# Walking the second MLP matrix in pairs of column blocks, and turning thirteen more tiles by DMA

## The chip, the cores and the metric

The kernel runs on one core of a Trainium2 chip. The metric is the time of one execution on the device in microseconds; the kernel before has a median of 1602.38 us over 3 runs (1599.79 to 1604.03). One more execution was taken with the hardware profiler, and its rows are what is quoted here. In them PE is the matmul engine (PEld its weight load), DVE the vector engine, ACT the scalar engine, POOL GpSimd, and SP the engine that issues most DMAs.

## The reference

One decoder block on x of 256 rows by 2048 columns, in float32:

```python
h = rms_norm(x, ln1_g[l])
proj = h @ w_in[l]                    # split into 12 parts
o_attn = dsa_attention(aq, ak, av, iq, ik, iw, topk)      # aq, ak: rms_norm per head
o_ret = silu(rg) * group_norm_heads(retention_chunkwise(...))
merged = sigmoid(ga) * (o_attn @ w_up_attn[l]) + sigmoid(gb) * (o_ret @ w_up_ret[l])
x = x + merged @ w_out[l]
h2 = rms_norm(x, ln2_g[l])
x = x + square(relu(h2 @ w_ff1[l])) @ w_ff2[l]
```

w_ff1 is 2048 x 8192 and w_ff2 is 8192 x 2048. The attention has 16 query heads and 4 key heads of 128 columns, and each query keeps the 64 keys of the highest indexer score.

## The kernel before

**Products.** Every float32 product is made of three matmuls on a high and a low part: high x high (L406), high x low part of the weights (L407), low part of the activations x high (L408). The weights come from HBM by DMA in tiles of 1 MB (`raw`, `rawc`), issued by SP, are rounded to the high part by ACT (`whi`, L360), and DVE subtracts to get the low part (`wlo`, L361). The activations are split likewise, after they have been transposed: ACT L430 writes the high, DVE L431 the low part of four 128x128 blocks at a time into the pair `act` that PE reads.

**Two ways to transpose.** `transpose_in` puts four 128x128 blocks of a tile through PE with an identity (L463) into a PSUM bank, and splits from there. `turn_in` calls `turned`: ACT copies the tile into two planes of 16 bits (L441), SP issues a transposing DMA from SBUF to SBUF (L443), and ACT copies the planes back together (L447); then the tile is split. `heads_T` (L557) turns keys and queries on PE. Each of these is a generator in a work list; `step()` is called once per item of the products and advances every generator in the list by one `yield`, so `wait` and `land` in the code count items.

**The MLP.** The 8192 columns of w_ff1 are taken in 8 groups (`NG`) of 1024. The first product of a group is formed, from group 1 on, with seven half-size products in place of eight (two levels of sums of weight tiles, which DVE adds in place: L350, the table `SUMS`), and is written to `pq` banks; its seven products have four items each. The second product (w_ff2, F2) of group g-1 runs in between: 16 items, for four column blocks `i` of 512 by two halves `h` by two steps `s`; an F2 item is 12 matmuls, a first-product item 6. `merged(g)` makes the list: one F2 item after every two items of the first product. An F2 block collects in two `pf` banks (one for each of the two row tiles t). At its last item ACT evicts each bank with a scale into a tile `ev` (L1261, two buffers), and POOL issues a DMA that adds it to `sums` in HBM (L1262). `F2_HALVES = (1, 0)`: of each block the half with the tiles (t, 1) comes first, then that of the tiles (t, 0).

A group makes four tiles (t, i), t and i 0 or 1, each squared after a relu by `squared` (L1178, L1179). `hidden(g, t, i)` puts them into the work list: in groups 1 to 6 the tiles (0,1), (1,1) and (0,0) go by `turn_in` and (1,0) by `transpose_in`; in group 7 (0,0) goes by `transpose_in` too; in group 0 all four do.

**The order.** The program is written in one order; a planner with costs for each instruction sets the order of each engine's instructions, and pools of a fixed number of buffers set what may be in flight.

Of the kernel before, what the change touches and what calls it, by code (L numbers as in the profile page):

```python
# [10 lines left out]
F32 = mybir.dt.float32  # L11
# [3 lines left out]
AF = mybir.ActivationFunctionType  # L15
# [3 lines left out]
P = 128  # L19
D = 2048  # L20
S = 256
T = S // P
DK = D // P
BN = 512
# [9 lines left out]
KC, HC = 4, 2  # L34
FG = 8
NG = DFF // (FG * P)
# [84 lines left out]
F2_HALVES = (1, 0)  # L121


def merged(g):

    f = iter([("F2", g - 1, i, h, s) for i in range(D // BN) for h in F2_HALVES for s in range(KC // HC)])
    out = []
    for n, p in enumerate(ORDER):
        for h in range(HK // KC):
            out += [("Q", g, n, h, s) for s in range(KC // HC)]  # L130
            if g > 1 or (n, h) > (0, 0):
                out.append(next(f))
        if p == 4:
            out.append(next(f))
    return out + list(f)
# [25 lines left out]
def block_kernel(ctx, tc, cst, rot, xt, gains, w, x, ret_gn_g, ret_gn_b, out):  # L161
    nc = tc.nc
# [9 lines left out]
    ep = tc.alloc_tile_pool(name="ep", bufs=1, side="right", reuse_waits="tile")  # L172
# [16 lines left out]
    banks(**ONE)  # L189


    W_NORM, W_SOFT, W_GN, W_CROSS, W_LATE = 3, 5, 7, 8, 10
    n_stg, n_mid, n_sm = 8, {"ep": 12, "e4": 20}, 24
    late = {"ep": ep, "stg": ep}
    n_stage = [0]
# [1 line left out]
    def nm(s):  # L197
        uid[0] += 1
        return f"{s}_{uid[0]}"

    def stage(shape=(P, BN)):
        n_stage[0] += 1
        pool, bufs = (late["stg"], 2) if n_stage[0] % 4 == 0 and "stg" in late else (sp, n_stg - 2)
        return pool.tile(list(shape), F32, tag="stg", name=nm("stg"), bufs=bufs)

    def mid(shape, dtype=F32):
        return late["ep"].tile(list(shape), dtype, tag="mid", name=nm("mid"), bufs=n_mid[late["ep"].name])

    def small(w):
        return sp.tile([P, w], F32, tag="small", name=nm("small"), bufs=n_sm)  # L210

    def psum_t():
        return PS["pt"].tile([P, BN], F32, tag="pt", name=nm("pt"))
# [8 lines left out]
    work = []  # L222
# [14 lines left out]
    gq, gk = gT[:, 2 * DK:2 * DK + 1], gT[:, 2 * DK + 1:2 * DK + 2]  # L237
# [32 lines left out]
    for g in range(1, NG):  # L270
        use += merged(g)
# [142 lines left out]
    def rsqrt(v, n, mul):  # L414

        a, y, u = small(n), small(n), small(n)
        nc.vector.tensor_scalar(a, v, mul, EPS, op0=ALU.mult, op1=ALU.add)
        nc.vector.tensor_scalar(y.bitcast(I32), a.bitcast(I32), -0.5, float(0x5F3759DF), op0=ALU.mult, op1=ALU.add)
        for _ in range(3):
            nc.vector.tensor_tensor(u, y, y, op=ALU.mult)  # L420
            nc.vector.scalar_tensor_tensor(u, u, -0.5, a, op0=ALU.mult, op1=ALU.mult)
            nc.vector.scalar_tensor_tensor(y, u, 1.5, y, op0=ALU.add, op1=ALU.mult)
        return y

    def split_into(act, k0, nk, t, ps):

        src = ps.rearrange("p (c i) -> p c i", c=nk)
        hi = act[0][:, k0:k0 + nk, t * P:(t + 1) * P]
        lo = act[1][:, k0:k0 + nk, t * P:(t + 1) * P]
        nc.scalar.activation(hi, src, AF.Copy)  # L430
        nc.vector.tensor_tensor(lo, src, hi.bitcast(F32), op=ALU.subtract)  # L431

    def interleaved(a):
        return a.bitcast(U16).rearrange("p (j h) -> p h j", h=2)

    def planes(a):
        return a.bitcast(U16).rearrange("p (h j) -> p h j", h=2)

    def turned(src, halves, wait):

        nc.scalar.activation(planes(halves), interleaved(src), AF.Copy)  # L441
        yield
        nc.sync.dma_start_transpose(src.bitcast(U16).rearrange("p (c r) -> p c r", r=P), halves.bitcast(U16))  # L443
        for _ in range(wait):
            yield
        with tc.issue_after(late["split"]):
            nc.scalar.activation(interleaved(halves), planes(src), AF.Copy)  # L447

    def turn_in(act, k0, t, src, tile_for, wait, land=W_CROSS):

        for _ in range(wait):
            yield
        halves = tile_for((P, BN))
        yield from turned(src, halves, land)
        split_into(act, k0, 4, t, halves)

    def transpose_in(act, k0, t, src, wait=2):

        for _ in range(wait):
            yield  # L460
        ps = psum_t()
        for c in range(4):
            nc.tensor.transpose(ps[:, c * P:(c + 1) * P], src[:, c * P:(c + 1) * P], ident)  # L463
        split_into(act, k0, 4, t, ps)
# [19 lines left out]
    psK, psI = ([PS["pm"].tile([P, BN], F32, tag="pm", name=nm("pm")) for _ in range(T)] for _ in range(2))  # L484
# [14 lines left out]
    def evict(dst, ps, t, func=AF.Copy):  # L499
        nc.scalar.activation(dst, ps, func, scale=rows[t])  # L500

    def evicted(ps, t):
        a = stage()
        evict(a, ps, t)
        return a
# [28 lines left out]
    def row_heads(tiles):  # L534

        hs = small(4 * T)
        for t, a in enumerate(tiles):
            sq = stage()
            nc.scalar.activation(sq, a, AF.Square)
            nc.vector.tensor_reduce(hs[:, 4 * t:4 * t + 4], sq.rearrange("p (h d) -> p h d", h=4), axis=AX.X, op=ALU.add)  # L540
        yield
        r = rsqrt(hs, 4 * T, 1.0 / HD)
        yield
        for t, a in enumerate(tiles):
            av = a.rearrange("p (h d) -> p h d", h=4)
            nc.vector.tensor_tensor(av, av, r[:, 4 * t:4 * t + 4].unsqueeze(2).to_broadcast([P, 4, HD]), op=ALU.mult)
        return tiles

    def heads_T(norm, dsts, g, wait):

        tiles = yield from norm
        for _ in range(wait):
            yield
        for t, a in enumerate(tiles):
            pst = psum_t()
            for h in range(4):
                nc.tensor.transpose(pst[:, h * P:(h + 1) * P], a[:, h * P:(h + 1) * P], ident)  # L557
            pst, dst = pst.rearrange("p (h i) -> p h i", h=4), dsts[t]
            if isinstance(dst, list):
                nc.scalar.activation(dst[0], pst, AF.Copy, scale=g)  # L560
                nc.vector.scalar_tensor_tensor(dst[1], pst, g, dst[0].bitcast(F32), op0=ALU.mult, op1=ALU.subtract)
            else:
                nc.scalar.activation(dst, pst, AF.Copy, scale=g)
            yield

    kT = ep.tile([P, NKV, S], F32, tag="kT", name="kT")
    vv = px.tile([P, 2, T, NKV * HD], F32R, tag="big2", name="vv")
    work.append(heads_T(row_heads([evicted(psK[t], t) for t in range(T)]), [kT[:, :, t * P:(t + 1) * P] for t in range(T)], gk, 2 * W_NORM))

    iqs = ep.tile([P, T, IW], F32, tag="big", name="iqs")  # L570
    for i in range(3):
# [84 lines left out]
    scale = HD ** -0.5  # L656
# [259 lines left out]
    for gate, u in ((z, u) for z in BESIDE for u in range(2)):  # L916
# [10 lines left out]
        for item in beside(gate, u):  # L927
# [7 lines left out]
            else:  # L935
                branch(item, of(oT if gate == "GA" else hT))
                i = item[0][1] - 2 * u
# [87 lines left out]
    for j in range(4):  # L1025
        if j < 2:

            i = j
# [5 lines left out]
        for src in (ret_gn_g, ret_gn_b):  # L1034
            g = mid([P, BN])
# [35 lines left out]
    for i in range(4):  # L1071
        ms = mss[i] if i in pair else gates(i)
        ps = run_block(("UR", i), of(rT), ps=pair.get(i), k0=len(PARTS[0]) * KC if i in pair else 0)
        for t, m in enumerate(ms):
            g = sgb[:, t, i * BN:(i + 1) * BN]
# [106 lines left out]
    def put(*new):  # L1182
        for (t, i), z, src in new:
            ys[t, i] = squared(z, src)
        for (t, i), _, _ in new:
            hidden(g, t, i)
# [3 lines left out]

    def hidden(g, t, i):
        act, y = [z[:, g % 2 * FG:] for z in hid[:2]], ys.pop((t, i))
        if g and (i or t == 0 and g < NG - 1):
            wait, room = ((1, 3)[t], spread) if i else (2, stage)
            work.append(turn_in(act, 4 * i, t, y, room, wait, W_LATE))
        else:
            work.append(transpose_in(act, 4 * i, t, y, 4 if g and (t, i) == (1, 0) else 2))

    def spread(shape):
        return late["f2"].tile(list(shape), F32, tag="stg", name=nm("halves"), bufs=2)  # L1200
# [3 lines left out]
    for i in (1, 0):  # L1204
        ps = run_block(("F1", i), lambda k, t: form(blocks[k // HK][t], k % HK))
        for t in range(T):
            ys[t, i] = squared(stage(), ps[t])
            if i:
                hidden(0, t, i)
# [58 lines left out]
    for t in range(T):  # L1268
        hidden(0, t, 0)
    for g in range(1, NG):  # L1270
        b, e = {}, {}
        for item in merged(g):
            if item[0] == "F2":
                second(item)
            else:
                first(item, b, e, form, put)
# [37 lines left out]
```

## Time and profile before

| what | value |
|---|---|
| median of 3 runs | 1602.38 us |
| profiled execution | 1600.71 us, span 1598.9 us |
| granted TensorE clock | 1.000 |
| PE busy | 1591.0 us |
| PE weight load busy | 1316.9 us |
| DVE busy | 1308.4 us (82%) |
| ACT busy | 1077.8 us (67%) |
| POOL busy | 90.6 us |
| HBM | 219 GB/s over the span |

The page of the profile gives for each engine the busy time and its share of the span, then the span in 40 slices, the DMA queues, the chain that ended last, and the costliest groups of instructions: line, engine, operation, tile written <- tiles read, shape, count, then busy time, mean duration in ns, and idle time of the engine before them with its releaser. The timelines have one row an instruction: start and duration in us, engine, line, operation and tiles. PE's matmuls overlap in their pipeline, so what one costs is read from start to start, and not from its duration.

### The profile page before, as it was taken

What the parts mean: (1) busy time and instruction counts of PE and PEld (TensorE: products, weight loads), DVE (VectorE), ACT (ScalarE), POOL (GpSimd) and SP (SyncE); (2) the same over time, 40 slices, a digit from 0 to 9 for tenths busy, and PEclk for the clock granted to TensorE, in tenths of its full rate; (3) what the DMA queues carried; (4) which work ended last, traced back from release to release, by engine and by line L of the source; (5) the groups of instructions that cost most, each with busy time, mean ns of one, the idle gap of its engine ahead of it and who ended that gap; (6) DMA issues with size and microseconds to landing.
All of it is one profiled execution on the core that took longest, in us unless ns stands there. A gap on an engine that the chain in (4) does not pass through costs nothing.

```text
span 1598.9 us, 19614 instructions
## 1 busy us (share of the span) xinstructions
PE 1591.0 (100%) x7294; PEld 1316.9 (82%) x7294; DVE 1308.4 (82%) x1466; ACT 1077.8 (67%) x1382; POOL 90.6 (6%) x135
## 2 busy tenths in 40 slices
PE   9999999999999999999999999999999999999999
PEld 8978888888888888888888888888887878888887
DVE  6678779898989898688575589898989898989884
ACT  7556766766566666466574666777878786868672
POOL 0000000000000001202000000000000000000000
PEclk9999999999999999999999999999999999999999
DMA  9645347856565755877666574878787777878773
GB/s 329 220 155 182 135 155 241 263 224 232 196 256 206 268 194 182 323 222 276 212 238 247 198 274 146 261 202 269 216 254 216 249 242 237 256 237 257 215 214 136
DMA packets 106432, 361.23 MB, mean 226 GB/s; under 512 B 45792, under 2 KB 52576, under 8 KB 70752
## 3 DMA queue, kind: packets, MB, share of 16 engines
q1 hardware_dynamic: 89056, 318.40, 56.8%
q0 software_dynamic: 14256, 35.14, 10.4%
q10 hardware_dynamic: 3024, 6.44, 1.1%
q8 instruction: 57, 0.93, 0.2%
q14 instruction: 39, 0.32, 0.1%
HBM read 323.24 MB, written 27.26 MB: 219 GB/s over the span
## 4 chain that ended last, share of the span: by engine, by line
PE 87%; DVE 8%; issue 2%; ACT 2%; DMA 1%; ACTq 0%; DVEq 0%
PE pm L407 11%; PE pm L408 11%; PE pm L406 11%; PE pf L407 9%; PE pf L408 9%; PE pf L406 9%; PE pq L407 7%; PE pq L408 7%; PE pq L406 7%; DVE wlo L361 4%; DVE raw L350 3%; ACT whi L360 1%; DMA rawc<-in_w_dram 1%; ACT halves L447 1%; DVE act L431 1%
## 5 line engine op out<-in xcount | busy, mean ns | idle before, releaser
L361 DVE TENSOR_TENSOR wlo<-raw,whi 128x1024 fp32r<-128x1024 f32 (+2 forms) x544 | 643.9, 1201 | 202.3 <-ACT whi L360 194.5
L360 ACT ACTIVATE whi<-raw 128x1024 fp32r<-128x1024 f32 (+2 forms) x544 | 561.3, 1042 | 348.2 <-PE pm L408 159.3
L406 PE MATMUL pm<-whi,act 128*128 128x512 f32 (+1 forms) x800 | 308.9, 387 | 1.5 <-ACT act L474 1.5
L407 PE MATMUL pm<-wlo,act 128*128 128x512 f32 (+1 forms) x800 | 306.9, 384 | 0.2 <-DVE wlo L361 0.2
L408 PE MATMUL pm<-whi,act 128*128 128x512 f32 (+1 forms) x800 | 307.1, 384 | 0.0
L407 PE MATMUL pf<-wlo,act 128*128 128x512 f32 (+1 forms) x768 | 299.0, 389 | 0.5 <-DVE wlo L361 0.5
L408 PE MATMUL pf<-whi,act 128*128 128x512 f32 (+1 forms) x768 | 298.6, 389 | 0.0
L406 PE MATMUL pf<-whi,act 128*128 128x512 f32 (+1 forms) x768 | 298.2, 390 | 0.4 <-ACT act L430 0.3
L361 DVE TENSOR_TENSOR wlo<-rawc,whi 128x1024 fp32r<-128x1024 f32 x176 | 215.0, 1221 | 41.2 <-ACT whi L360 39.0
L360 ACT ACTIVATE whi<-rawc 128x1024 fp32r<-128x1024 f32 x176 | 186.2, 1058 | 73.7 <-PE pf L408 35.1
L350 DVE TENSOR_TENSOR raw<-raw,raw 128x2048 f32<-128x2048 f32 x88 | 201.1, 2287 | 0.5
L406 PEld LDWEIGHTS pm<-whi,act 128*128 128x128 f32 x800 | 150.3, 188 | 28.2 <-ACT act L474 1.7
L408 PEld LDWEIGHTS pm<-whi,act 128*128 128x128 f32 x800 | 150.4, 188 | 27.9 <-DVE act L475 0.2
L407 PEld LDWEIGHTS pm<-wlo,act 128*128 128x128 f32 x800 | 150.5, 188 | 27.7 <-DVE wlo L361 1.9
L407 PEld LDWEIGHTS pf<-wlo,act 128*128 128x128 f32 x768 | 144.2, 188 | 31.7 <-DVE wlo L361 2.7
L406 PEld LDWEIGHTS pf<-whi,act 128*128 128x128 f32 x768 | 143.7, 188 | 32.3 <-ACT whi L360 2.3
L408 PEld LDWEIGHTS pf<-whi,act 128*128 128x128 f32 x768 | 144.2, 188 | 31.6 <-DVE act L431 2.2
L407 PE MATMUL pq<-wlo,xf 128*128 128x512 f32 x392 | 153.2, 391 | 0.8 <-DVE wlo L361 0.8
L406 PE MATMUL pq<-whi,xf 128*128 128x512 f32 x392 | 152.8, 390 | 0.0
L408 PE MATMUL pq<-whi,xf 128*128 128x512 f32 x392 | 152.6, 389 | 0.0
L1262 POOL DMA_DIRECT2D sums<-ev x56 | 48.1, 936 | 757.1 <-ACT ev L1261 755.4
L407 PEld LDWEIGHTS pq<-wlo,xf 128*128 128x128 f32 x392 | 73.6, 188 | 18.3 <-DVE wlo L361 3.2
(223 smaller groups left out, 1575.0 us busy)
## 6 DMA issues: line engine op xcount, KB each, us to landing
raw<-in_w_dram SPq DMA_DIRECT2D x188, 1024.0 KB, 5.5
rawc<-in_w_dram SPq DMA_DIRECT2D x88, 1024.0 KB, 5.2
sums<-ev POOLq DMA_DIRECT2D x56, 256.0 KB, 5.3
raw<-in_w_dram SPq DMA_DIRECT2D x8, 736.0 KB, 4.9
raw<-in_w_dram SPq DMA_DIRECT2D x7, 512.0 KB, 7.0
raw<-in_w_dram SPq DMA_DIRECT2D x8, 368.0 KB, 7.4
stg<-in_x_dram SPq DMA_DIRECT2D x8, 256.0 KB, 7.6
mgd<-stg POOLq DMA_DIRECT2D x8, 256.0 KB, 5.8
```

Of the source, the lines that this page charges most:

```text
L350: nc.vector.tensor_tensor(one, one, two, op=ALU.add)
L360: late["split"] = nc.scalar.activation(a, src, AF.Copy).ins
L361: nc.vector.tensor_tensor(b, src, a.bitcast(F32), op=ALU.subtract)
L406: nc.tensor.matmul(d, h, hi, start=first, stop=False, skip_group_check=skip)
L407: nc.tensor.matmul(d, h, lo, start=False, stop=False, skip_group_check=skip)
L408: nc.tensor.matmul(d, l, hi, start=False, stop=last, skip_group_check=skip)
L431: nc.vector.tensor_tensor(lo, src, hi.bitcast(F32), op=ALU.subtract)
L447: nc.scalar.activation(interleaved(halves), planes(src), AF.Copy)
L1262: nc.gpsimd.dma_start(sums[:, t, i * BN:(i + 1) * BN], z, accum_op=ALU.add)
```

## The change

Three things are changed. `merged` walks the column blocks of F2 in pairs: for two blocks first both halves of the tiles (t, 1), then both of the tiles (t, 0), so four `pf` banks are open at once, and blocks end with the 6th, 8th, 14th and 16th F2 item instead of the 4th, 8th, 12th and 16th. The half h = 0 of a group is first read by the 5th F2 item instead of the 3rd. `hidden` sends all tiles but (1,0) of group 7 through `turn_in`, with new waits and new numbers of items for the landing. The two key tiles go through `turned` in a new pair of generators. In all, 52 PE transposes (13 sets of four) go; 26 ACT copies and 13 transposing DMAs on SP come.

```diff
-    f = iter([("F2", g - 1, i, h, s) for i in range(D // BN) for h in F2_HALVES for s in range(KC // HC)])
+    f = iter([("F2", g - 1, i + a, h, s) for i in range(0, D // BN, 2) for h in F2_HALVES for a in range(2) for s in range(KC // HC)])
...
-    W_NORM, W_SOFT, W_GN, W_CROSS, W_LATE = 3, 5, 7, 8, 10
+    W_NORM, W_SOFT, W_GN, W_CROSS = 3, 5, 7, 8
...
-    work.append(heads_T(row_heads([evicted(psK[t], t) for t in range(T)]), [kT[:, :, t * P:(t + 1) * P] for t in range(T)], gk, 2 * W_NORM))
+
+    def key_heads(tiles):
+
+        yield from row_heads(tiles)
+        for _ in range(W_NORM):
+            yield
+        for t, a in enumerate(tiles):
+            work.append(key_tile(t, a))
+
+    def key_tile(t, a):
+
+        for _ in range(2 * t):
+            yield
+        halves = ep.tile([P, BN], F32, tag="halves", name=nm("halves"), bufs=2)
+        yield from turned(a, halves, W_CROSS)
+        nc.scalar.activation(kT[:, :, t * P:(t + 1) * P], halves.rearrange("p (h i) -> p h i", h=4), AF.Copy, scale=gk)
+
+    work.append(key_heads([evicted(psK[t], t) for t in range(T)]))
...
         act, y = [z[:, g % 2 * FG:] for z in hid[:2]], ys.pop((t, i))
-        if g and (i or t == 0 and g < NG - 1):
-            wait, room = ((1, 3)[t], spread) if i else (2, stage)
-            work.append(turn_in(act, 4 * i, t, y, room, wait, W_LATE))
-        else:
-            work.append(transpose_in(act, 4 * i, t, y, 4 if g and (t, i) == (1, 0) else 2))
+        if g == NG - 1 and (t, i) == (1, 0):
+            work.append(transpose_in(act, 4 * i, t, y, 4))
+            return
+        wait, room, land = (1 + 2 * t, spread if g or not i else stage, 10 if not g else 7)
+        if g and not i:
+            wait, room, land = ((2, stage, 15), (1, spread, 11))[t] if g < NG - 1 else (1, stage, 7)
+        work.append(turn_in(act, 4 * i, t, y, room, wait, land))
```

The planner sets the order of each engine anew. Two places are shown, both at the start of an MLP group in the middle (the profile of before has it at 1214 us).

ACT, before: the splits of weights (`whi`) of the first items, the copies (L447) and splits (L430) of the tiles (0,1) and (1,1), one relu and square (L1178, L1179), and the evictions (`ev`) of the last block.

```order
L360 ACTIVATE whi_10726<-raw_10651 128x1024
L447 ACTIVATE halves_10566<-stg_10449 128x2x512
L360 ACTIVATE whi_10742<-raw_10651 128x1024
L430 ACTIVATE act_7813<-halves_10566 128x4x128
L1178 ACTIVATE stg_10537<-stg_10537 128x512
L1179 ACTIVATE stg_10537<-stg_10537 128x512
L360 ACTIVATE whi_10758<-rawc 128x1024
L447 ACTIVATE halves_10596<-stg_10289 128x2x512
L1261 ACTIVATE ev_10777<-pf_10657,q_7814 128x512
L430 ACTIVATE act_7813<-halves_10596 128x4x128
L1261 ACTIVATE ev_10780<-pf_10658,q_7814 128x512
L360 ACTIVATE whi_10784<-raw_10695 128x1024
```

The same place after (lines are moved: the relu is L1195 and the square L1196, the eviction L1280; the first L447 and its L430 stand just ahead of these rows, with the first eviction):

```order
L1280 ACTIVATE ev_10705<-pf_10494,q_7812 128x512
L360 ACTIVATE whi_10710<-rawc 128x1024
L447 ACTIVATE halves_10589<-stg_10279 128x2x512
L360 ACTIVATE whi_10723<-raw_10638 128x1024
L430 ACTIVATE act_7811<-halves_10589 128x4x128
L1195 ACTIVATE stg_10528<-stg_10528 128x512
L360 ACTIVATE whi_10736<-raw_10638 128x1024
L1196 ACTIVATE stg_10528<-stg_10528 128x512
L360 ACTIVATE whi_10752<-rawc 128x1024
L441 ACTIVATE halves_10756<-stg_10528 128x1024
L1280 ACTIVATE ev_10770<-pf_10559,q_7812 128x512
L1280 ACTIVATE ev_10773<-pf_10560,q_7812 128x512
```

The next row is `whi_10777`, which answers to `whi_10784` before. Ahead of it there are now two pairs of evictions instead of one, and the first copy (L441) of the tile (1,0).

DVE, before: the adds (L350), the splits of weights (`wlo`, L361), and the low parts of the tiles (1,0) (from the PSUM bank `pt`) and (0,0) (from `stg_10687`), both L431:

```order
L350 TENSOR_TENSOR raw_10714<-raw_10714,raw_10843 128x2048
L361 TENSOR_TENSOR wlo_10785<-raw_10695,whi_10784 128x1024
L361 TENSOR_TENSOR wlo_10799<-raw_10695,whi_10798 128x1024
L361 TENSOR_TENSOR wlo_10809<-rawc,whi_10808 128x1024
L431 TENSOR_TENSOR act_7813<-pt_10812,act_7813 128x4x128
L361 TENSOR_TENSOR wlo_10834<-raw_10651,whi_10833 128x1024
L361 TENSOR_TENSOR wlo_10846<-raw_10651,whi_10845 128x1024
L361 TENSOR_TENSOR wlo_10858<-rawc,whi_10857 128x1024
L350 TENSOR_TENSOR raw_10695<-raw_10695,raw_10795 128x2048
L431 TENSOR_TENSOR act_7813<-stg_10687,act_7813 128x4x128
L350 TENSOR_TENSOR raw_10795<-raw_10795,raw_10889 128x2048
L361 TENSOR_TENSOR wlo_10879<-raw_10695,whi_10878 128x1024
```

DVE after, from the third of these adds on (here (0,0) comes from `stg_10675` and (1,0) from `halves_10756`):

```order
L350 TENSOR_TENSOR raw_10708<-raw_10708,raw_10830 128x2048
L361 TENSOR_TENSOR wlo_10863<-raw_10683,whi_10862 128x1024
L361 TENSOR_TENSOR wlo_10876<-raw_10683,whi_10875 128x1024
L361 TENSOR_TENSOR wlo_10886<-rawc,whi_10885 128x1024
L350 TENSOR_TENSOR raw_10789<-raw_10789,raw_10873 128x2048
L361 TENSOR_TENSOR wlo_10904<-raw_10830,whi_10903 128x1024
L361 TENSOR_TENSOR wlo_10915<-raw_10830,whi_10914 128x1024
L431 TENSOR_TENSOR act_7811<-stg_10675,act_7811 128x4x128
L361 TENSOR_TENSOR wlo_10930<-rawc,whi_10929 128x1024
L350 TENSOR_TENSOR raw_10830<-raw_10830,raw_10638 128x2048
L431 TENSOR_TENSOR act_7811<-halves_10756,act_7811 128x4x128
L361 TENSOR_TENSOR wlo_10950<-raw_10873,whi_10949 128x1024
```

Between two adds there are three splits now, where two adds stood with one L431 between; the two L431 come later, behind the fourth and behind the fifth add.

## The prediction

> **What bounds the kernel now.** I read the page first (busy shares, the slices, the chain, the groups), then the waits of PE, then windows of one MLP group, then timelines inside it.
>
> ```profile
> span 1598.9 us, 19614 instructions
> PE 1591.0 (100%) x7294; PEld 1316.9 (82%) x7294; DVE 1308.4 (82%) x1466; ACT 1077.8 (67%) x1382; POOL 90.6 (6%) x135
> DVE  6678779898989898688575589898989898989884
> PE 87%; DVE 8%; issue 2%; ACT 2%; DMA 1%; ACTq 0%; DVEq 0%
> L361 DVE TENSOR_TENSOR wlo<-raw,whi 128x1024 fp32r<-128x1024 f32 (+2 forms) x544 | 643.9, 1201 | 202.3 <-ACT whi L360 194.5
> L350 DVE TENSOR_TENSOR raw<-raw,raw 128x2048 f32<-128x2048 f32 x88 | 201.1, 2287 | 0.5
> ```
>
> PE is busy 1591.0 of 1598.9 us: a matmul less is time less, as long as nothing else paces PE at that place. DVE is at 82%, and its slices alternate between 8 and 9 in the second half: there are stretches where it is full. What PE waits for by the waits view is little:
>
> ```profile
> PE pq L407 <- DVE wlo L361: 0.8, 5, 0.2
> PE pf L407 <- DVE wlo L361: 0.5, 1, 0.5
> ```
>
> Five waits, one in each of five MLP groups. The windows show the stretch they belong to (columns: length, then busy time and count of PE, weight load, DVE, ACT, POOL; granted clock; DMA share; GB/s):
>
> ```profile
> 1130.90:1169.00 38.10, 37.94 (x168) 30.57 (x167) 38.10 (x30) 29.09 (x34) 3.40 (x4) 1.00 0.69 216
> 1169.00:1214.00 45.00, 45.00 (x200) 37.09 (x199) 36.17 (x33) 35.29 (x41) 3.45 (x4) 1.00 0.88 264
> ```
>
> For the first 38 us of a group DVE does not rest at all, and in the other 45 it has 8.8 us to spare. The chain of waits between 1147 and 1154 us says the same from the other side:
>
> ```profile
> 1148.39 0.69 DVE act L431
> 1149.08 2.20 DVE raw L350
> 1151.28 1.15 DVE wlo L361
> 1152.42 0.04 issue
> 1152.47 0.50 PE pq L407
> ```
>
> So **two clocks** run here: PE's nearly everywhere, DVE's in the first 38 us of every MLP group. What a group loses to DVE today is seen in PE's timeline, from start to start:
>
> ```profile
> 1148.55 0.39 PE L407 MATMUL pf<-wlo,act 128*128 128x512 f32 x1
> 1148.77 0.39 PE L406 MATMUL pf<-whi,act 128*128 128x512 f32 x1
> ...
> 1152.47 0.50 PE L407 MATMUL pq<-wlo,xf 128*128 128x512 f32 x1 [0.16 <-DVE wlo L361]
> 1152.80 0.39 PE L408 MATMUL pq<-whi,xf 128*128 128x512 f32 x1
> ```
>
> The first two rows are 0.22 to 0.23 us apart, the usual spacing (0.227 in the mean). From 1148.77 to 1152.80 PE makes 14 such steps in 4.03 us; 14 x 0.227 is 3.18. The **0.86 us** between is the loss, and groups 1 to 6 each have such a place.
>
> **What the change removes.** 52 PE transposes in 13 sets of four. What one set costs on PE:
>
> ```profile
> L463 PE MATMUL pt<-csb,stg 128*128 128x128 f32 x64 | 9.5, 272 | 0.0
> L557 PE MATMUL pt<-csb,stg 128*128 128x128 f32 x40 | 7.2, 284 | 0.0
> 1136.72 0.39 PE L408 MATMUL pq<-whi,xf 128*128 128x512 f32 x1
> 1136.95 0.60 PE L463 MATMUL pt<-csb,stg 128*128 128x128 f32 x4
> 1137.31 0.48 PE L406 MATMUL pf<-whi,act 128*128 128x512 f32 x1
> 1137.62 0.40 PE L407 MATMUL pf<-wlo,act 128*128 128x512 f32 x1
> ...
> 1138.55 0.39 PE L408 MATMUL pf<-whi,act 128*128 128x512 f32 x1
> ```
>
> From the L408 at 1136.72 to the L408 at 1138.55 are 1.83 us with six matmul starts between; six at 0.227 us would be 1.36, so a set costs **0.46 us**, not the 4 x 0.272 us of its busy time. Thirteen sets: 13 x 0.455 = **-5.9 us**, of which the keys' two are 0.9, group 0's four 1.8, the sets of groups 1 to 6 are 2.75, the one of group 7 is 0.45.
>
> **What it adds.** Per tile two ACT copies and one transposing DMA on SP:
>
> ```profile
> L441 ACT ACTIVATE halves<-stg x24: 1037/1042/1060, 263.0 to 1528.9; 128x1024 uint16<-128x1024 uint16 x24
> L447 ACT ACTIVATE halves<-stg x24: 1355/1362/1371, 273.5 to 1549.4; 128x1024 uint16<-128x1024 uint16 x24
> L443 SPq DMA_TRANSPOSE stg<-halves x24: 1232/1250/3721, 264.1 to 1530.4; - x24
> DMA to landing us min/median/max: 3.1/5.4/9.7
> ```
>
> 13 x (1.04 + 1.36) = 31 us of ACT, which is at 67% and has gaps; hidden as long as ACT does not stand just ahead of DVE in a full stretch. The DMA: SP is held 1.25 us, landing 5.4, at worst 9.7 us after issue. One step of the work list in a group is 83.1 us / 44 items = 1.9 us (the 38.1 and the 45.0 us of the two windows are one group), so the waits of 7, 10, 11 and 15 steps are 13 to 28 us: the landing is covered even at 9.7. For the keys, eight steps there (six matmuls each, 368 wide instead of 512, so 6 x 0.227 x 0.72 = 1.0 us, an estimate) are about 8 us: covered at the median, 2 us late at the worst, with nothing but a kT copy behind it. SP's weight loads move by 1.25 us per transpose; they are issued many items ahead. Both at 0. A rule of the Trainium skill speaks against the change: "VectorE: DVE Perf Modes", in its list for kernel authors, takes TensorE for a 128x128 transpose wherever a PSUM destination is fine, and its section on the three transpose paths gives TensorE 390 ns and the DMA 1309 ns. Charged in full, 0.92 us more for each of 52 transposes, that would make an estimate of +48 us in place of -5.9. The trace has the DMA route in use already, with PE busy beside it, so its duration is not charged here.
>
> **Keys: -0.9.** No full stretch is near; DVE stands at 6 to 7 tenths in the first slices.
>
> **Group 0: -1.8 + 1.5 = -0.3.** The first items of the merged order need the split of group 0's (1,0) and (1,1) tiles and the first weights at once. In the new order two L447 (1.23 us from start to start), two L430 and a relu-and-square pair stand ahead of the split of the fourth product's weights on ACT; walked with these durations, that split comes about 0.6 us late and the next two again, together 1.5 us. Bounds: 0 (the list's waits hold) and 3 (each of the two L447 passes on in full).
>
> **A group from 1 to 6: -0.46 + 0.3 = -0.15, six times -0.9.** This is the term that decides. ACT: the excerpts above show that the copy L441 (0.95 start to start) and two more evictions stand ahead of the split that follows the fourth weights of the group.
>
> ```profile
> L1261 ACT ACTIVATE ev<-pf,q x56: 654/688/692, 993.4 to 1551.7; 128x512 f32<-128x512 f32 x56
> 1130.89 1.23 DVE L361 TENSOR_TENSOR wlo<-raw,whi 128x1024 fp32r<-128x1024 f32 x1 [0.34 <-ACT whi L360]
> 1142.18 0.68 DVE L431 TENSOR_TENSOR act<-pt,act 128x512 fp32r<-128x512 f32 x1
> 1142.79 2.35 DVE L361 TENSOR_TENSOR wlo<-raw,whi 128x1024 fp32r<-128x1024 f32 x2
> 1145.05 1.22 DVE L361 TENSOR_TENSOR wlo<-rawc,whi 128x1024 fp32r<-128x1024 f32 x1
> 1146.19 2.28 DVE L350 TENSOR_TENSOR raw<-raw,raw 128x2048 f32<-128x2048 f32 x1
> ```
>
> An eviction is 0.56 us from start to start, so ACT has 0.95 + 2 x 0.56 = 2.1 us more to do there, and DVE, which starts its full stretch waiting for ACT (the 0.34 at 1130.89), starts 1.2 to 1.7 us later. Against that, DVE gets two things back. The L431 of (1,0) and of (0,0) leave the place between the adds (at 1142.18 and 1148.39 now): 0.6 us each, 1.2 together. And the adds stand apart: before, add, L431, add are 2.2 + 0.6 + 2.2 = 5.0 us without a split; after, three splits lie between two adds, 2.2 + 3 x 1.14 = 5.6 us for what PE eats in 5.4 (two products at 1.36 and one second-matrix item at 2.72): DVE falls back 0.2 per round, with no burst. So the 0.86 at the adds mostly goes. What comes in its place is **the L431 of (1,0)**, now behind the fifth add: by the walk it ends some 32 us into the group, and PE wants it at 31 in the fifth second-matrix item. 0.3 to 1.1 us; the order PE itself is given there has a single matmul pulled ahead, so the middle of that is enough: 0.7. With some 0.2 left at the adds and 0.3 for the evictions (next rival) a group loses 1.2 where it lost 0.86. Bounds: a group loses nothing any more (-1.3 with the set), or DVE is late by all of its 1.7 and the L431 by 1.1 (+1.5).
>
> **Group 1's tail +0.5, the end -0.75.** At the end of group 1's list the last two blocks of the pair end two items apart with no product between, so their pairs of evictions are 5.4 us apart; I take one wait of half a microsecond. At the end (0,0) of group 7 goes by DMA (-0.45), and its copy sits behind one split more; 0.5 where 0.82 is lost now (-0.3).
>
> **The sum**: -0.9 - 0.3 - 0.9 + 0.5 - 0.75 = -2.35 us on the profiled execution, 1600.71 us (its span is 1598.9). The median shown, 1602.38, is 1.7 above it, so the forecast is 1602.38 - 2.35 = **1600.0**.
>
> **Rivals.** *A: the sets go and nothing takes their place.* Speaks for it: ACT idles within the full stretch (29.1 of 38.1 us busy), so it could take the copies without delaying a split; two L431 fewer in that stretch. Against: ACT's gaps come after the first eight microseconds, not in them. Time: -5.9, and up to 6 x 0.86 = 5.2 more if the stalls go with it: 1591.5 to 1596.5, middle 1595.
>
> *B: the evictions hold ACT, slower.* They have two buffers, and each is free when its accumulating DMA has landed:
>
> ```profile
> L1262 POOL DMA_DIRECT2D sums<-ev x56: 842/852/1152, 994.4 to 1552.7; - x56
> DMA to landing us min/median/max: 4.0/5.3/14.4
> ```
>
> Today four pairs of evictions are spread over a group's 83.1 us, one about every 20 us, and 14.4 is covered. With two blocks ending two items apart the next pair comes 8 us after the last (the ACT rows between the two pairs above: four splits of 0.95, a 1.23, an L430, the 1.15 of relu and square, an L441 and the two evictions), in group 1's tail 5.4. A landing of 5.3 is covered, one of 10 holds ACT for 2 us, and ACT then holds the splits with DVE already full. From about 1.2 us of wait in each group the gain is gone; at 1.5 us in six groups: 1600.0 + 9 = **1609**. For it: the second DMA of a pair queues behind the first on POOL; against: 5.3 is the median. The Trainium skill, "Perfetto Trace Analysis", Optimization Strategy, takes a gap that repeats on the engine that should be full as a sign of too few buffers; the repeated 0.86 us of today follows a DVE split and not a buffer, so no row of before bears that out for the evictions.
>
> *C: the (1,0) landing or the keys' are late.* If SP gets to a transpose late (3.7 us once) and it lands at 9.7, (1,0)'s copy slips by a part of a step (1.9 us), 1 us in six groups: 1606. Against: 13 us or more are given.
>
> **How the numbers follow.** A measurement of this kernel tells about 0.3%, 4.8 us, from no change: faster is below 1597.6, slower above 1607.2. Forecast 0.42 (own range 1597 to 1604), A 0.33, B 0.18, C 0.07. Faster: 0.31 of A and 0.04 of the forecast's low side, 0.35. Slower: 0.17 of B, 0.03 of C and 0.03 of the forecast's high side, 0.23. No change 0.42. The range reaches from the upper half of A to below the middle of B: 1593 to 1607.
>
> **What would show it.** Right: no L463 or L557 for the moved tiles and PE's busy time down by 52 instructions; in the windows of the first 38 us DVE still full; PE's waits in a group now at an L408 of pf behind DVE act L431, not at L407 of pq. A is shown by waits of PE that sum to less than before; B by ev L1280 waiting for a DMA on ACT and whi behind it; C by L447 waiting for DMA. The forecast is wrong if the stretch's DVE has idle time (then A), or if a group's period is above 83.5 us (then B).

## The result: 1.0% slower

The changed kernel takes 1617.56 us (median of 5 runs, 1616.85 to 1621.74) against 1601.67 us before (5 runs); the ratio is 1.0102, with a 95% interval of 1.0086 to 1.0119. Forecast were 1600.0 and a range of 1593 to 1607. The profiled execution took 1616.85 us with a span of 1614.9, so 16.0 us of span are to be found. Times are medians over the undisturbed executions of a run; the run without half of the DMAs (e13) had one more, of 1909 us at a granted clock of 0.778, and with it its median would be 1596.0 in place of 1595.4.

### The profile page after: what moved, and what is told of

Read it like the earlier page. It is cut to its first block, busy times and chain, and to the rows that moved or that the text cites. A ratio compares the mean times of both kernels' runs of the same rounds, so it can differ in the third digit from the quotient of the medians.

```text
span 1614.9 us, 19564 instructions
## 1 busy us (share of the span) xinstructions
PE 1593.5 (99%) x7242; PEld 1314.4 (81%) x7242; DVE 1307.9 (81%) x1466; ACT 1101.7 (68%) x1408; POOL 90.5 (6%) x135
## 4 chain that ended last, share of the span: by engine, by line
PE 57%; issue 36%; DVE 3%; POOL 2%; DMA 2%; ACT 0%; POOLq 0%; ACTq 0%; DVEq 0%
PE pm L407 9%; PE pm L408 9%; PE pm L406 9%; PE pf L408 5%; PE pf L407 5%; PE pf L406 5%; PE pq L407 4%; PE pq L408 4%; PE pq L406 4%; POOL sums L1281 2%; DVE wlo L361 1%; DMA sums<-ev 1%; PE pa L406 1%; PE pa L408 0%; PE pa L407 0%
## 5 line engine op out<-in xcount | busy, mean ns | idle before, releaser
L361 DVE TENSOR_TENSOR wlo<-raw,whi 128x1024 fp32r<-128x1024 f32 (+2 forms) x544 | 643.0, 1200 | 218.4 <-ACT whi L360 212.9
L361 DVE TENSOR_TENSOR wlo<-rawc,whi 128x1024 fp32r<-128x1024 f32 x176 | 214.6, 1220 | 41.6 <-ACT whi L360 40.4
L360 ACT ACTIVATE whi<-rawc 128x1024 fp32r<-128x1024 f32 x176 | 185.8, 1056 | 59.1 <-PE pf L408 24.1
L350 DVE TENSOR_TENSOR raw<-raw,raw 128x2048 f32<-128x2048 f32 x88 | 201.0, 2285 | 0.6
L406 PE MATMUL pq<-whi,xf 128*128 128x512 f32 x392 | 155.0, 395 | 5.1 <-ACT whi L360 5.0
L408 PE MATMUL pq<-whi,xf 128*128 128x512 f32 x392 | 154.5, 394 | 0.0
L406 PEld LDWEIGHTS pq<-whi,xf 128*128 128x128 f32 x392 | 74.3, 190 | 24.0 <-ACT whi L360 7.8
```

The source lines that it names most:

```text
L350: nc.vector.tensor_tensor(one, one, two, op=ALU.add)
L360: late["split"] = nc.scalar.activation(a, src, AF.Copy).ins
L361: nc.vector.tensor_tensor(b, src, a.bitcast(F32), op=ALU.subtract)
L406: nc.tensor.matmul(d, h, hi, start=first, stop=False, skip_group_check=skip)
L408: nc.tensor.matmul(d, l, hi, start=False, stop=last, skip_group_check=skip)
```

## The profile after

The page, and the waits of PE and ACT:

```profile
span 1614.9 us, 19564 instructions
PE 1593.5 (99%) x7242; PEld 1314.4 (81%) x7242; DVE 1307.9 (81%) x1466; ACT 1101.7 (68%) x1408; POOL 90.5 (6%) x135
```

```profile
PE pf L408 <- DVE act L431: 5.2, 5, 1.4
PE pq L406 <- ACT whi L360: 5.0, 4, 1.7
PE pq L407 <- DVE wlo L361: 4.5, 6, 0.8
```

```profile
ACT ev L1280 <- DMA sums<-ev: 23.1, 13, 4.7
```

The 52 transposes are gone (7294 to 7242), and yet PE's busy time is longer. PE waits 14.7 us in these three rows, where its waits for splits in the groups were 1.3. And ACT, which before never waited for a DMA at an eviction, does so 13 times, for 23.1 us. Up to the middle nothing is lost: the first split of an attention tile after the key and query work starts at 703.9 us (first), where it started at 705.2 (second):

```profile
L430 ACT ACTIVATE act<-halves x26: 613/617/637, 703.9 to 1562.2; 128x512 fp32r<-128x512 f32 x26
```

```profile
L430 ACT ACTIVATE act<-halves x18: 612/616/634, 705.2 to 1551.2; 128x512 fp32r<-128x512 f32 x18
```

All of the loss lies in the MLP groups. ACT's timeline at the start of one, the same place of a group as in the excerpts of the section on the change, one group earlier:

```profile
1134.77 1.04 ACT L360 ACTIVATE whi<-rawc 128x1024 fp32r<-128x1024 f32 x1
1135.73 1.04 ACT L441 ACTIVATE halves<-stg 128x1024 uint16<-128x1024 uint16 x1
1138.20 0.69 ACT L1280 ACTIVATE ev<-pf,q 128x512 f32<-128x512 f32 x1 [1.44 <-DMA sums<-ev]
1141.77 0.69 ACT L1280 ACTIVATE ev<-pf,q 128x512 f32<-128x512 f32 x1 [2.88 <-DMA sums<-ev]
1142.36 1.99 ACT L360 ACTIVATE whi<-raw 128x1024 fp32r<-128x1024 f32 x2
```

ACT stands still for 4.3 us at the two evictions of the fourth block, and the splits of weights stand behind them. What PE does with that:

```profile
1141.41 0.39 PE L407 MATMUL pf<-wlo,act 128*128 128x512 f32 x1
1141.64 0.39 PE L408 MATMUL pf<-whi,act 128*128 128x512 f32 x1
1143.45 0.51 PE L406 MATMUL pq<-whi,xf 128*128 128x512 f32 x1 [1.43 <-ACT whi L360]
1144.71 0.79 PE L407 MATMUL pq<-wlo,xf 128*128 128x512 f32 x1 [0.76 <-DVE wlo L361]
1145.31 0.63 PE L408 MATMUL pq<-whi,xf 128*128 128x512 f32 x1
1145.73 0.63 PE L406 MATMUL pq<-whi,xf 128*128 128x512 f32 x1
1146.16 0.63 PE L407 MATMUL pq<-wlo,xf 128*128 128x512 f32 x1
```

It starts 1.6 us late for the high part and 1.0 late for the low one, and then its matmuls stand 0.43 us apart instead of 0.227, until 1147.5. The windows name that: the granted clock (the column ahead of the DMA share) is 0.57.

```profile
1058.00:1062.00 4.00, 3.97 (x11) 3.15 (x12) 4.00 (x4) 2.61 (x3) 0.00 (x0) 0.61 0.59 93
1144.00:1148.00 4.00, 3.29 (x9) 2.63 (x10) 4.00 (x4) 2.99 (x4) 0.00 (x0) 0.57 0.51 70
1404.00:1408.00 4.00, 4.00 (x12) 3.15 (x12) 4.00 (x4) 2.47 (x3) 0.00 (x0) 0.62 0.56 174
```

There are three such spells, each some eight steps by 0.2, about 1.6 us of PE's time. How late the DMA was is in the view of the evictions of 1127.5 to 1131 us, the pair that is waited for:

```profile
DMA to landing us min/median/max: 9.1/10.6/12.1
```

## The experiments

Three theories. **1**: the second block of a pair ends two items after the first, and its evictions wait for the accumulating DMAs of the first. **2**: the low part of tile (1,0) comes too late. **3**: the 26 new copies crowd ACT.

### The walk in pairs by itself

The kernel before with the new line in `merged`, and nothing else.

> The kernel before, with the second MLP matrix walked in pairs of column blocks and nothing else changed. Theory 1 (evictions: the second block of a pair ends two items after the first, and its evictions on ACT must wait until the accumulating DMA of the first has freed one of the two buffers; the splits of weights stand behind them): the waits of ACT ev for DMA appear here too, with no tile moved to the DMA, and PE waits for whi and wlo at group starts: 1608 to 1614 us. Theory 2 (what hurts is the low part of tile (1,0), made too late on DVE): that tile stays on PE here, so nothing is lost: 1600 to 1604. Theory 3 (the 26 new copies crowd ACT at the group starts): no copies here, so also 1600 to 1604.

1616.61 us, 1.0100 [1.0083, 1.0117]: as slow as the change, without one tile moved, and 2.6 us above what theory 1 gave.

```profile
ACT ev L1261 <- DMA sums<-ev: 20.8, 14, 3.8
```

Theories 2 and 3 can't make this, since there is no late tile and no copy in it.

### Three ways to take the wait away

Only the first two blocks as a pair:

```diff
-    f = iter([("F2", g - 1, i + a, h, s) for i in range(0, D // BN, 2) for h in F2_HALVES for a in range(2) for s in range(KC // HC)])
+    f = iter([("F2", g - 1, i + a, h, s) for i, n in ((0, 2), (2, 1), (3, 1)) for h in F2_HALVES for a in range(n) for s in range(KC // HC)])
```

> The changed kernel, with only the first two column blocks walked as a pair and the third and fourth one after the other, as before. Blocks end with the 6th, 8th, 12th and 16th item, so the evictions at a group's start stand alone, and the close pair falls in the middle, where DVE has time to spare. All new copies and transposing DMAs stay. Theory 1: most of the loss at group starts goes, 11 to 13 us of the 16; 1604 to 1607. Theory 2: (1,0) is no earlier, 1615 to 1618. Theory 3: the copies are still there, 1613 to 1618.

1598.39 us, 0.9983 [0.9974, 0.9992], better than expected. Evictions wait 1.9 us in all. What is left is one place in group 1, where weights come late:

```profile
ACT whi L360 <- DMA rawc<-in_w_dram: 7.8, 3, 6.7
ACT ev L1280 <- DMA sums<-ev: 1.9, 3, 1.0
```

Pairs as in the change, own room for the first and third block's evictions:

```diff
-    z = late["f2"].tile([P, BN], F32, tag="ev", name=nm("ev"), bufs=2)
+    z = late["f2"].tile([P, BN], F32, tag="ev", name=nm("ev"), bufs=2) if i % 2 else stage()
```

> The changed kernel with its pairs, but the evictions of the first and third block go into tiles of the general staging pool, so that the evictions of a pair's second block find their own two buffers free. Same work, same DMAs. Theory 1: waits of ACT ev for DMA fall from 23 us to under 5, the half-clock places in PE's matmuls go with them, 1603 to 1608. Theory 2 and theory 3: 1613 to 1618.

1595.12 us, 0.9963 [0.9948, 0.9978], 8 us below the expected range: not only is the loss gone, the kernel is faster than before. The place of the stall, now:

```profile
1131.55 1.05 ACT L441 ACTIVATE halves<-stg 128x1024 uint16<-128x1024 uint16 x1
1132.50 1.26 ACT L1280 ACTIVATE ev<-pf,q 128x512 f32<-128x512 f32 x2
1133.63 2.01 ACT L360 ACTIVATE whi<-raw 128x1024 fp32r<-128x1024 f32 x2
```

Three buffers (`bufs=3`, and `n_stg` 7 instead of 8 to make room):

> The changed kernel with three buffers for the evictions instead of two (and one buffer fewer in the staging pool, to make room). Theory 1 (an eviction waits until the accumulating DMA has freed its buffer): with three, the first eviction of a close block finds a free one and only the second waits, for a DMA that was issued first of its pair and lands some 3 us earlier than the one it waits for with two; waits of ACT ev for DMA between the 23 us of two buffers and the none of the run with its own room, 5 to 12 us, and the time between these two, 1598 to 1608. If the staging pool and not the number of eviction buffers was what helped in the run with its own room: 1613 or more.

1598.29 us, 0.9983 [0.9974, 0.9992]. Waits of evictions: 23.1 us with two buffers, 6.3 with three, none with own room; times 1617.6, 1598.3, 1595.1.

```profile
ACT ev L1280 <- DMA sums<-ev: 6.3, 4, 4.1
```

These runs also change which staging tiles are shared, so the last one takes only the DMA away (the sums of the first and third block are then missing from its output):

```diff
-    nc.gpsimd.dma_start(sums[:, t, i * BN:(i + 1) * BN], z, accum_op=ALU.add)
+    if i % 2: nc.gpsimd.dma_start(sums[:, t, i * BN:(i + 1) * BN], z, accum_op=ALU.add)
```

> The changed kernel, with two eviction buffers and everything else as it is, but the accumulating DMAs of the first and third column block are left out for groups 0 to 6 (so those blocks' sums are not in the output). The evictions of a pair's second block then find buffers that nothing reads. Theory 1: no waits of ACT ev for DMA, no spells of half clock, PE's waits for whi at group starts gone, 1594 to 1598. If the crowding of ACT by copies, and not the wait, makes the loss: 1610 or more.

1595.41 us, 0.9965 [0.9950, 0.9979], as expected of theory 1, with the granted clock at 1.000 over the span. ACT's evictions wait for PE alone, and the stall at the group's start is gone from its timeline:

```profile
ACT ev L1280 <- PE pf L408: 10.5, 14, 1.0
```

```profile
1131.81 1.05 ACT L441 ACTIVATE halves<-stg 128x1024 uint16<-128x1024 uint16 x1
1132.76 1.26 ACT L1280 ACTIVATE ev<-pf,q 128x512 f32<-128x512 f32 x2
1133.90 2.01 ACT L360 ACTIVATE whi<-raw 128x1024 fp32r<-128x1024 f32 x2
```

Tiles, buffers and staging pool are those of the change here, and ACT's and DVE's instructions come in the same order. Half the accumulating traffic went with the wait, but the run with own room has all of it and is as fast. Theory 1 stands: 1617.6 - 1595.4 = 22.2 us (21.4 between the two profiled spans).

### Does the room help by itself?

Controls: the same own room in the kernel before, and under the walk in pairs alone.

> Control: the kernel before, with the evictions of the first and third block in tiles of the staging pool, as in the run of the changed kernel with its own room. Before, no eviction waited for a DMA in the trace, so theory 1 expects no gain here: 1599 to 1603, and the 1595 of the changed kernel with its own room is then the change's own. If it falls to 1595 to 1597 too, that room helps whatever the order, and the change is worth nothing.

1605.93 us, 1.0033 [1.0021, 1.0045]. Slower, which was not expected: the staging tiles that the evictions now hold are wanted elsewhere, and ACT waits for them at another copy.

```profile
ACT stg L441 <- DMA sums<-stg: 15.6, 6, 7.0
```

So room is no gain of its own.

> The walk in pairs alone (no tile moved to the DMA), with the evictions of the first and third block in tiles of the staging pool. With the runs before it this makes a square: order of blocks by eviction room. Theory 1: the whole loss of the pairs alone (1616.6) goes with the room, 1600 to 1605, about what the kernel before has with the same room (1605.9) or a little less. If the pairs also cost something by themselves (the order of adds and splits, four open banks): 1608 or more.

1606.48 us, 1.0047 [1.0028, 1.0066]. The square in us: before 1601.7, pairs 1616.6, room 1605.9, pairs and room 1606.5. With the room the pairs cost no more than the room alone. But this run does not take the wait away: five evictions now wait for a borrowed tile (first row), and five of PE's matmuls stand late behind a split (second row). Each of the five starts 7.45 us after an eviction that had waited, whether that wait was 1.7 or 3.1 us; the last two rows show one such place. So the square does not show what the pairs cost where no eviction waits, nor what the moved tiles add: with pairs, room and tiles (1595.1) these evictions wait for no DMA.

```profile
ACT stg L1261 <- DMA sums<-stg: 10.6, 5, 3.1
PE pf L407 <- DVE wlo L361: 6.7, 5, 1.4
1130.13 0.69 ACT L1261 ACTIVATE stg<-pf,q 128x512 f32<-128x512 f32 x1 [1.80 <-DMA sums<-stg]
1137.58 0.50 PE L407 MATMUL pf<-wlo,act 128*128 128x512 f32 x1 [1.36 <-DVE wlo L361]
```

### The late tile (1,0)

On PE again in groups 1 to 6 (`if g and (t, i) == (1, 0)` for `if g == NG - 1 and ...`):

> The changed kernel, with tile (1,0) of groups 1 to 6 transposed on PE as before. Theory 2: PE's waits for DVE act L431 (5.2 us, with the late steps around them some 7) go, the six sets cost 2.75 again: 1612 to 1614. Theory 1: the evictions still wait, so no more than that: 1612 to 1616. Theory 3: 12 of the 26 copies leave the group starts, 1606 to 1610.

1616.20 us, 1.0094 [1.0079, 1.0109]. No more than the change itself: evictions wait even longer, 41.0 us.

Copied back one item earlier (`(1, spread, 10)` for `(1, spread, 11)`), with own room and then without:

> The changed kernel with its own room for evictions, and the tile (1,0) of groups 1 to 6 copied back one item earlier (landing after 10 items instead of 11), which puts its low part on DVE ahead of the fifth add instead of behind it. With its own room, PE still loses 0.6 us in each of five groups at the L408 that waits for this low part (theory 2's place). Theory 2: these 3 us go, 1591 to 1593.5. If another split is then late in its place: 1594 to 1596.

1600.84 us, 1.0001 [0.9992, 1.0010], a miss: 5.7 us slower than with 11 items. Without the edit (own room, 11 items) PE waits for the low part, and its steps there are 0.6 us late in sum at each of five places (first fence). With it the copy stands ahead of ACT's L893, which empties the `pq` bank that the next product needs, and PE is 1.2 us late there (second, PE; third, ACT), again at five places. That is 3 of the 5.7 us; four more waits of PE between 1053 and 1078 us, 1.8 us in sum, are new in this run:

```profile
1157.88 0.39 PE L406 MATMUL pf<-whi,act 128*128 128x512 f32 x1
1158.60 0.50 PE L408 MATMUL pf<-whi,act 128*128 128x512 f32 x1 [0.34 <-DVE act L431]
```

```profile
1156.12 0.39 PE L408 MATMUL pf<-whi,act 128*128 128x512 f32 x1
1157.53 0.50 PE L406 MATMUL pq<-whi,xf 128*128 128x512 f32 x1 [1.03 <-ACT stg L893]
```

```profile
1153.43 1.36 ACT L447 ACTIVATE stg<-stg 128x1024 uint16<-128x1024 uint16 x1
1154.66 1.35 ACT L447 ACTIVATE halves<-stg 128x1024 uint16<-128x1024 uint16 x1
...
1156.90 0.58 ACT L893 ACTIVATE stg<-pq 128x512 f32<-128x512 f32 x1
```

> The changed kernel with two eviction buffers, and only the tile (1,0) copied back one item earlier. Theory 2 by itself: PE's waits for DVE act L431 (5.2 us) and the late steps beside them go, 7 us, 1610 to 1612. If they are a result of theory 1 (ACT late, so DVE late, so everything that follows in the full stretch late), the wait moves to a split of weights and 1614 to 1618 stays.

1623.23 us, 1.0140 [1.0123, 1.0156], a miss too: 5.7 us worse than the change, the same 5.7 as with own room. Theory 2's wait is real and small, and one item earlier moves it to a worse place.

### In search of a better version

> The changed kernel with its own room for evictions and tile (1,0) of groups 1 to 6 on PE. Six sets cost 2.75 us more, the five stalls of 0.6 us at the low part of (1,0) go, 3 us, and 12 copies leave ACT: 1594 to 1596, no different from the 1595.1 with the tile on the DMA. If the DMA route of this tile is worth its 0.46 us a group: 1597 to 1598.

**1593.97 us, 0.9957 [0.9944, 0.9970]**, the best of all. With the room, PE's five waits go once (1,0) is on PE. In the full stretch of a group DVE is as full as ever, and PE has no gap left:

```profile
1214.00:1252.00 38.00, 38.00 (x171) 31.44 (x171) 38.00 (x29) 27.73 (x31) 3.45 (x4) 1.00 0.57 183
```

> The changed kernel with three eviction buffers and tile (1,0) of groups 1 to 6 on PE. With three buffers alone 6.3 us of waits were left and 1598.3; with own room, the tile on PE was 1.2 us better than on the DMA. 1595 to 1600; if the remaining waits for the second eviction fall where DVE is full, the upper end.

1595.98 us, 0.9967 [0.9955, 0.9978], with one staging tile fewer and none borrowed.

> Search for the best version: the changed kernel, only the first two blocks as a pair, and own room for the first and third block's evictions. By theory 1 neither change needs the other, so the room adds nothing where evictions wait 1.9 us in sum: 1592 to 1599, the lower end if the load of weights that came 6.7 us late once in group 1 is in time here.

1610.62 us, 1.0060 [1.0047, 1.0074], a miss by 12 us: in this order the borrowed tiles are waited for, 19.6 us on ACT, and two spells at a lower clock follow (0.54 between 1048 and 1052 us, 0.71 between 1220 and 1224).

```profile
ACT stg L441 <- DMA sums<-stg: 19.6, 6, 6.5
```

> The kernel before, its walk of blocks unchanged, with the part of the moved tiles that does not need the pairs: the keys' two, group 0's (0,1) and (1,1), and (0,0) of group 7: 5 sets of 0.455 us, 2.3 us less of PE. If a set taken from PE outside the full stretches is worth its full 0.455: 1598.5 to 1600. If the copies on ACT give it back: 1601 to 1602.

1602.57 us, 1.0007 [0.9996, 1.0017]. Five sets of transposes less, and no gain: a small miss. The profiled execution, at the upper end (1605.2), has ACT waiting up to 4.2 us for weights in group 1 and a clock of 0.50 just behind it, between 1056 and 1060 us, and the runs scatter from 1599.5 to 1605.5; whether all of the 2.3 us went there is open.

## Why the prediction was wrong

**The step that failed** is the price of the evictions: 0.3 us a group in "A group from 1 to 6", and 0.5 once in group 1's tail. Measured, the wait costs 22.2 us, the difference between the change and the same kernel without the DMAs that are waited for. It lies at six places, 3.7 us each: group 1's tail at 1053 us and five group starts. Without it my sum would have been 1602.38 - 2.35 - 1.8 - 0.5 = 1597.7; the kernels without the wait took 1595.1 and 1595.4. So the mechanism that I had as rival B, at a chance of 0.18, was right in place and direction, and two of its numbers were wrong.

First, the size of the wait. I held 5.3 us, the median of all 56, against the 8 us between two close pairs. But an eviction waits for its own buffer's DMA, and a pair that issues within a microsecond lands at 9.1 and 12.1 us in the place that counts. At the six places the later of the two landed after 8.7 to 12.1 us. The 14.4 in the same quoted row, of the pair at 1035 us in group 1's list, was the warning; I went by the median of a row of which six places decide. Their waits came to 22.1 us, 3.7 each, where rival B had 1.5 (a seventh, of 1.0 at 1566 us, costs nothing). Second, the chance: I took the median as evidence against.

That ACT's wait passes on to PE in full, as rival B had it, is borne out place by place. The matmul that wants the low part of (1,0) starts at these times in five groups of the change:

```profile
1167.21 0.50 PE L408 MATMUL pf<-whi,act 128*128 128x512 f32 x1 [0.69 <-DVE act L431]
1253.44 0.51 PE L408 MATMUL pf<-whi,act 128*128 128x512 f32 x1 [1.37 <-DVE act L431]
1338.53 0.50 PE L408 MATMUL pf<-whi,act 128*128 128x512 f32 x1 [1.38 <-DVE act L431]
1424.95 0.50 PE L408 MATMUL pf<-whi,act 128*128 128x512 f32 x1 [0.40 <-DVE act L431]
1510.37 0.50 PE L408 MATMUL pf<-whi,act 128*128 128x512 f32 x1 [1.38 <-DVE act L431]
```

Without the DMAs that are waited for it starts at 1158.86, 1241.29, 1323.73, 1406.16 and 1488.56 us. From one group to the next the change falls back by 3.8, 2.7, 4.0 and 3.0 us, and the evictions before these four starts had waited 3.7, 2.6, 3.9 and 2.9. The spells at half clock, which I had not foreseen, add nothing to that: 4.0 against 3.9 in the group with the one at 1404, 3.8 against 3.7 in one without. DVE's split at 1143.43 is 8.3 us later than without the DMAs before the spell begins, and the matmul at 1167.21 is 8.35 later behind it; PE only waits less for the low part behind a spell (0.69 and 0.40 against 1.37 and 1.38).

Both signs named for B came: the splits behind an eviction that waits for a DMA, and a period above 83.5 us (85.1 to 86.4 between the rows). But not every wait counts in full: with (1,0) on PE the evictions waited 41.0 us, and the kernel was 22.2 us slower than with own room (1616.2 and 1594.0). A small slip in rival A: its low end, 1602.38 - 5.9 - 5.2, is 1591.3 and not 1591.5.

**Right:** the keys (-0.9 forecast; 1.3 us gained at 705 us) and the set's price: two sets of group 0 later, at the first matmul into `pq`, 2.2 us are gained (965.88 against 968.11). Group 0 (-0.3): the 60 us from 940 hold 273 matmuls before and 258 after, and 16 of the 273 were transposes, so one matmul's worth, 0.2 us, is gained.

```profile
940.00:1000.00 60.00, 60.00 (x273) 49.33 (x272) 51.89 (x42) 38.77 (x46) 1.78 (x2) 1.00 0.61 211
```

```profile
940.00:1000.00 60.00, 59.61 (x258) 47.61 (x258) 50.99 (x41) 45.23 (x52) 0.00 (x0) 1.00 0.73 221
```

The low part of (1,0) as the wait in place of those at the adds: forecast 0.7 us a group; 0.6 where no eviction waits. That the DMA's landing is covered for the transposes (rival C) held: PE, ACT and DVE show no wait for one of them. Rival A was half right: with the wait gone the stalls of 0.86 do go (the windows row of the run with own room and (1,0) on PE, where PE waits 0.3 us in all groups together), but my 1595 for it needed a buffer that the change doesn't have. The end's -0.75 was not measured by itself.

The Trainium skill ("Perfetto Trace Analysis", Optimization Strategy) takes a gap that repeats on the saturated engine as a possible sign of too few buffers. I set that aside because no row of before showed it. The rows after do: ACT waits for a buffer's DMA at the starts of the groups, PE has its gap behind it, and one more buffer takes most of it away.

## What to carry to other kernels

Where a change brings two users of a double buffer closer together, hold the new interval against the latest landing of the pair in the place where it matters, not against the median of all of them. A wait on an engine that is 68% busy counted in full here where the engine behind it had no slack; look for the stretch, not the share. And a room that is borrowed from a shared pool has its own waits: measure it in the kernel before as well.

## What the runs showed of the hardware that was not expected

TensorE's granted clock fell to about half after waits that were short in themselves. At 1143 us two waits, 1.6 and 1.0 us late with one matmul between, were followed by steps of 0.43 us (1.4 and 0.8 in the waits' own count); the same happened at 1058, behind waits of 1.7 and 0.8, and at 1404, behind 1.0 and 0.8. But size alone doesn't decide. In the run of pairs alone two places with the same two waits (1.4 and 0.8 us) end differently, one at 0.57 and one at 1.00:

```profile
1399.00:1403.00 4.00, 4.00 (x12) 3.16 (x11) 4.00 (x5) 2.58 (x5) 0.00 (x0) 0.57 0.43 100
1487.00:1491.00 4.00, 4.00 (x19) 3.28 (x19) 4.00 (x5) 4.00 (x7) 0.00 (x0) 1.00 0.49 111
```

The Trainium skill, "TensorE: Matmul & The Clock Gate", Part 1, describes a free-running window in which the activity is watched; two equal waits could then end differently by where they fall in it. The spacing at half clock agrees with the page (426.7 ns for 512 columns; 0.43 here). That the window is the cause was not tested.
